# The subtractions that make the low parts of the HGRN weights, on VectorE in place of GpSimd

## The chip, the cores and the metric

One Trainium2 chip, of which the kernel uses one core. A core has five engines: TensorE (PE in the profile; PEld is its weight load), VectorE (DVE), ScalarE (ACT), GpSimd (POOL) and SyncE (SP), which issues most of the DMAs. Each takes its instructions in a fixed order. The metric is the device time of one execution in microseconds. Before the change it was 1303.19 us, the median of three runs.

## The reference

One layer of a hybrid decoder on 1024 tokens of width 1024. An RMS norm, one input projection, two groups of heads (8 HGRN heads of width 128, a gated linear recurrence; 16 FoX heads of width 64, softmax attention with a forget gate), a SiLU gate on each group, an output projection, a gated per-layer input, and a last norm.

```python
u = rmsnorm(h, norm_w[i])
proj = jnp.einsum('bsd,de->bse', u, w_in[i])
hq, hf, hi, hg, fq, fk, fv, fg, fz = jnp.split(proj, SPLIT_POINTS, axis=-1)
y_h = hgrn2_branch(hq, hf, hi, lb_all[i], hgrn_gn[i]) * jax.nn.silu(hg)
y_f = fox_branch(fq, fk, fv, fz, fox_fb[i]) * jax.nn.silu(fg)
h = h + jnp.einsum('bse,ed->bsd', jnp.concatenate([y_h, y_f], axis=-1), w_out[i])
ple = jnp.einsum('bsk,kd->bsd', p[i], w_ple[i])
h = h + jax.nn.sigmoid(jnp.einsum('bsd,de->bse', h, w_ple_gate[i])) * ple
```

`hgrn2_branch` keeps for each head a 128 x 128 state, S_t = diag(f_t) S_{t-1} + k_t i_t^T, with k = 1 - f, and reads it with q.

## The kernel before

**Products in split precision.** Each projection is a product of fp32 values in which both factors are split into a high part (rounded to the type fp32r) and a low part, and three of the four products of parts are summed: high x high, high x low, low x high. The helper `split` (L82, L83) makes the two parts of a tile: ScalarE casts the tile to its high part, then a second engine, given by the caller, subtracts that from the tile and so makes the low part. `load_w` (L88 the DMA) loads one tile of weights, 128 x 1024 fp32 (512 KB), into `wf` and splits it into `whi` and `wlo`; `load_pair` (L145) loads two such tiles for the values of a pair of heads into `wf` and splits them into the halves of `wthi` and `wtlo`. The tags `wf`, `whi` and `wlo` have two buffers each, `wthi` and `wtlo` one. So the cast of a tile waits until PE has done its last product with the tile two before, and the DMA of a tile waits until an earlier `wf` has been subtracted.

**The order of the loads** is written out in `w_in_loads`, a generator of closures: first the HGRN tiles (for each head f, q and g, with a pair of value tiles after every second head), then the FoX tiles, then the first tile of the output projection. `Ahead.weights()` hands out the tile that is loaded and starts the load of the next one, so each tile is loaded while the tile before it is multiplied. The numbers of the tiles are T_HQ 0 to 7, T_HF 8 to 15, T_HI 16 to 23, T_HG 24 to 31, and from T_FQ = 32 on the FoX tiles; a negative number stands for a pair. The first f tile and the first pair of value tiles are loaded elsewhere, in the start stage, by `load_w` and by `split_pair`, both with GpSimd.

**The HGRN stage** (about 55 to 520 us). For each of eight heads, `hgrn_mix` does the recurrence by blocks, and between its steps PE works ahead on the next head's projections: `ahead.fill(n)` runs so many columns of the jobs that are queued (`product_steps`, L371, the matmuls of 512 or 256 columns). PE's order is fixed as written (`pe` is `tc.keep_in_program_order`); the order on the other engines is made by the scheduler when the program is built, by what is ready and by the order of writing. The steps of a head that the prediction names:

- L579: PE's small matmuls for the scores of a group. L590, L591 and L621: VectorE copies them under a mask out of PSUM.
- L587, L596, L597, L614, L615, L635: VectorE scales the queries (`x`) for the next radix; L599, L645, L678, L681: it scales `k` and the queries. L599 and L645 stand ahead of the next scores (L579, then L661 and L673), L681 ahead of PE's transposes of `k` (L699). L633 is a copy on ScalarE.
- L699, L707, L726: PE transposes `k`, multiplies it with the values and makes the output; L711 and L713: VectorE's chain of states; L689: GpSimd copies the scores of the smallest blocks into `st`.
- L549, L552, L558 and L559: the projections for f, q and g leave PSUM; L559, on VectorE, multiplies the gate and frees the buffer. L562, L563: VectorE makes k and f from the sigmoid. L536: VectorE copies the values of one block out of PSUM. The projections have two PSUM buffers (the tag `proj`).
- L751 and L753: PE transposes a head's output and VectorE gates it.

Then comes the FoX stage (to about 1010 us), whose tiles are also loaded by `load_w` with GpSimd, and the output projection, whose tiles are split with VectorE.

Of the kernel before, what the change touches and what calls it, by code (L numbers as in the profile page):

```python
# [20 lines left out]
KT = D // P  # L21
CH = 512
NCH = S // CH
HEADS_H = 8
# [14 lines left out]
T_HQ, T_HF, T_HI, T_HG, T_FQ, T_FK, T_FV, T_FG = (8 * i for i in range(8))  # L39
# [25 lines left out]
def trunk(ctx: ExitStack, tc: tile.TileContext, a, out):  # L65
    nc = tc.nc
# [14 lines left out]
    def split(hi, lo, src, lo_engine, pin=lambda ins: ins):  # L81
        pin(nc.scalar.copy(hi, src))  # L82
        pin(lo_engine.tensor_tensor(out=lo, in0=src, in1=hi, op=ALU.subtract))  # L83

    def load_w(src, k, lo_engine=None, pin=lambda ins: ins):

        wf = wpool.tile([P, KT, P], F32, name="wf", tag="wf", bufs=2)
        nc.sync.dma_start(out=wf[:, :k], in_=src)  # L88
        hi = wpool.tile([P, KT, P], F32R, name="whi", tag="whi")
        lo = wpool.tile([P, KT, P], F32R, name="wlo", tag="wlo")  # L90
        split(hi[:, :k], lo[:, :k], wf[:, :k], lo_engine or nc.gpsimd, pin)
        return hi, lo
# [47 lines left out]
    def load_pair(tile0):  # L140

        whi, wlo = (wt.tile([P, KT, 2 * P], F32R, name=name) for name in ("wthi", "wtlo"))
        for i in range(2):
            wf = wpool.tile([P, KT, P], F32, name="wf", tag="wf", bufs=2)
            nc.sync.dma_start(out=wf, in_=a["w_in"][tile0 + i])  # L145
            sl = slice(i * P, (i + 1) * P)
            split(whi[:, :, sl], wlo[:, :, sl], wf, nc.gpsimd)
        return whi, wlo

    def token_major(w, v, blocks, evac_pin=lambda ins: ins):  # L150
# [232 lines left out]
    def w_in_loads():  # L383
        tiles = [T_HQ, T_HG]
        for h in range(HEADS_H - 1):
            tiles += [T_HF + h + 1, T_HQ + h + 1, T_HG + h + 1] + ([-(h + 2)] if h % 2 == 0 and h < HEADS_H - 2 else [])
        tiles += [T_FQ, T_FG, T_FK, T_FV]
        for p in range(PAIRS_F - 1):
            tiles += [T_FK + p + 1, T_FQ + p + 1] + ([T_FG + p] if 0 < p < FIRST_LATE else []) + [T_FV + p + 1]
        tiles += [T_FG + p for p in range(FIRST_LATE, PAIRS_F)]  # L390
        for t in tiles:
            yield (lambda t=t: load_w(a["w_in"][t], KT)) if t >= 0 else (lambda t=t: load_pair(T_HI - t))
        yield lambda: load_w(a["w_out"][0], KT, nc.vector)

    ahead = Ahead(w_in_loads(), first_f)


# [110 lines left out]
    with ExitStack() as st:  # L508
# [8 lines left out]
        for i in range(2):  # L517
            t = hs.tile([P, FB, P], F32, name=f"st{i}")
            nc.gpsimd.memset(t, 0.0)
            st_t.append(t)  # L520
            t = hs.tile([P, FB, 32], F32, name=f"r{i}")
# [261 lines left out]
    with fox as st:  # L783
# [219 lines left out]
        for c in range(NCH):  # L1003
            sl = slice(c * CH, (c + 1) * CH)
# [167 lines left out]
```

## Time and profile before

| what | us |
|---|---|
| time before, median of 3 runs (lowest, highest) | 1303.19 (1299.52, 1303.29) |
| the profiled execution's own time | 1302.99 |
| its span, from its first instruction to its last | 1301.2 |
| HGRN stage, 55 to 520 us: busy VectorE / ScalarE / GpSimd | 281.3 / 120.1 / 100.4 |
| FoX stage, 520 to 1010 us: busy PE / VectorE / GpSimd | 486.2 / 331.8 / 175.1 |

How to read the rows below. A row of the timeline gives the start in us, the duration in us, the engine, the line of the kernel, the operation, the tiles (out<-in), the shape, and how many instructions were merged (x2); in brackets the idle time of the engine just before and what ended it. A row of the waits gives who waited for whom: us in total, number of times, the longest in us. A row of a stretch gives from:to, its length and then the busy us of PE, PEld, DVE, ACT and POOL with the count of instructions, the granted share of PE's clock, the busy share of the DMA engines and GB/s. Durations in rows of a line (min/median/max) are in ns. A matmul's duration in the profile is longer than its step, since the next one starts before it ends; steps are read from start to start.

### The profile page before, as it was taken

The numbers are of one execution on the slowest core, as the hardware profiler recorded it, in microseconds if no ns is written. First come the engines' busy times: TensorE is split into PE (matmuls) and PEld (weight loads), VectorE is DVE, ScalarE is ACT, GpSimd is POOL, SyncE is SP. The second block draws the span as 40 slices with busy tenths as digits, with TensorE's granted clock in tenths as the row PEclk, the third lists the DMA queues.
The fourth block names the chain that finished last, engine by engine and source line by source line (L and its number), as shares of the span: only waits on it lengthen the run. The fifth ranks groups of instructions, "written<-read, shape, count | busy, mean of one in ns | idle before, by whom it ended". The sixth has DMA issues, their size and how long they took to land.

```text
span 1301.2 us, 26821 instructions
## 1 busy us (share of the span) xinstructions
PE 1263.7 (97%) x10996; PEld 1010.5 (78%) x10996; DVE 783.8 (60%) x1986; ACT 480.1 (37%) x1170; POOL 348.9 (27%) x288
## 2 busy tenths in 40 slices
PE   7998999999999999999999999999999999999996
PEld 5977888888788877777777777776766788888895
DVE  6555575755657486377666666667777633333465
ACT  6423132212313224255444444444545312222454
POOL 3522123212211112424343434242432100002232
PEclk9999999999999999999999999999999999999998
DMA  7411111101111020222122222211241652212321
GB/s 297 145 35 64 50 33 66 50 34 49 50 50 50 18 67 19 82 66 83 58 75 59 74 64 70 72 59 58 82 139 59 234 171 89 81 49 85 116 76 65
DMA packets 38971, 102.23 MB, mean 79 GB/s; under 512 B 6720, under 2 KB 8896, under 8 KB 38848
## 3 DMA queue, kind: packets, MB, share of 16 engines
q1 hardware_dynamic: 38704, 99.99, 23.2%
q8 instruction: 86, 1.41, 0.5%
q0 software_dynamic: 144, 0.52, 0.1%
q14 instruction: 37, 0.30, 0.1%
HBM read 83.07 MB, written 17.43 MB: 77 GB/s over the span
## 4 chain that ended last, share of the span: by engine, by line
PE 82%; DVE 7%; ACT 5%; DMA 2%; issue 2%; POOL 1%; SPq 0%; DVEq 0%; ACTq 0%; POOLq 0%
PE ps L371 47%; PE lg L828 5%; PE ps L100 5%; PE ps L98 5%; PE ps L99 5%; PE po L876 5%; ACT x L864 2%; PE ps L579 1%; PE gps L100 1%; PE gps L98 1%; PE gps L99 1%; DVE x L842 1%; PE po L724 1%; PE po L726 1%; PE pk L707 1%
## 5 line engine op out<-in xcount | busy, mean ns | idle before, releaser
L371 PE MATMUL ps<-uhi,whi 128*128 128x512 f32 x896 | 361.0, 403 | 0.0
L371 PE MATMUL ps<-ulo,whi 128*128 128x512 f32 x896 | 354.8, 396 | 0.0
L371 PE MATMUL ps<-uhi,wlo 128*128 128x512 f32 x896 | 353.1, 394 | 0.0
L83 POOL TENSOR_TENSOR wlo<-wf,whi 128x1024 fp32r<-128x1024 f32 x59 | 145.0, 2457 | 441.6 <-ACT whi L82 425.6
L371 PEld LDWEIGHTS ps<-uhi,whi 128*128 128x128 f32 x896 | 168.5, 188 | 58.4 <-issue 22.5
L371 PEld LDWEIGHTS ps<-uhi,wlo 128*128 128x128 f32 x896 | 168.9, 188 | 35.9 <-issue 1.1
L371 PEld LDWEIGHTS ps<-ulo,whi 128*128 128x128 f32 x896 | 168.8, 188 | 33.7 <-issue 0.7
L864 ACT ACTIVATE x<-x,mxo 128x512 f32<-128x512 f32 (+15 forms) x256 | 130.4, 512 | 66.0 <-DVE mxo L852 66.0
L82 ACT CAST whi<-wf 128x1024 fp32r<-128x1024 f32 (+1 forms) x77 | 79.7, 1036 | 202.2 <-PE ps L99 89.8
L842 DVE CUSTOM_DVE_ANT_0 x<-lg,fb 128x512 f32<-128x512 f32 (+15 forms) x256 | 101.8, 433 | 73.4 <-PE lg L828 66.6
L865 DVE STREAM_TRANSPOSE pt<-x 128x512 f32<-128x512 f32 (+15 forms) x256 | 115.1, 458 | 39.8 <-ACT x L864 35.9
L98 PE MATMUL ps<-yhi,whi 128*128 128x512 f32 x256 | 99.8, 390 | 1.7 <-DVE h L1024 1.7
L99 PE MATMUL ps<-ylo,whi 128*128 128x512 f32 x256 | 99.7, 389 | 0.3 <-DVE ylo L83 0.3
L100 PE MATMUL ps<-yhi,wlo 128*128 128x512 f32 x256 | 99.6, 389 | 0.0
L828 PE MATMUL lg<-k,q 64*32 64x480 f32 (+15 forms) x1024 | 74.9, 396 | 2.6 <-DVE mx L842 2.6
L828 PE MATMUL lg<-k,qx 64*32 64x512 f32 (+15 forms) x1024 | 74.9, 396 | 1.2 <-DVE mx L842 1.2
L876 PEld LDWEIGHTS po<-pt,v 64*64 64x64 f32 x1536 | 53.6, 133 | 22.7 <-issue 9.2
L876 PE MATMUL po<-pt,v 64*64 64x256 f32 (+7 forms) x1536 | 69.4, 320 | 0.0
L98 PEld LDWEIGHTS ps<-yhi,whi 128*128 128x128 f32 x256 | 48.0, 188 | 12.0 <-ACT whi L82 2.1
L99 PEld LDWEIGHTS ps<-ylo,whi 128*128 128x128 f32 x256 | 48.0, 188 | 10.7 <-DVE ylo L83 0.7
L100 PEld LDWEIGHTS ps<-yhi,wlo 128*128 128x128 f32 x256 | 48.1, 188 | 10.1
L371 PE MATMUL ps<-wthi,uhi 128*128 128x256 f32 x192 | 54.0, 281 | 0.0
(209 smaller groups left out, 2131.4 us busy)
## 6 DMA issues: line engine op xcount, KB each, us to landing
wf<-in_w_in_dram SPq DMA_DIRECT2D x64, 512.0 KB, 3.5
fb<-fd SPq DMA_DIRECT2D x64, 128.0 KB, 3.1
yf<-yd SPq DMA_DIRECT2D x16, 512.0 KB, 5.3
wf<-in_w_out_dram SPq DMA_DIRECT2D x16, 512.0 KB, 3.6
x<-in_xT_dram SPq DMA_DIRECT2D x8, 512.0 KB, 9.7
pled<-pleo SPq DMA_DIRECT2D x16, 256.0 KB, 3.0
yd<-sg SPq DMA_DIRECT2D x8, 512.0 KB, 2.6
rz<-zd SPq DMA_DIRECT2D x16, 256.0 KB, 3.4
```

The costliest lines, as they stand in the source:

```text
L82: pin(nc.scalar.copy(hi, src))
L83: pin(lo_engine.tensor_tensor(out=lo, in0=src, in1=hi, op=ALU.subtract))
L98: pin(mm(ps, whi, uhi, start=i == 0, stop=False))
L99: pin(mm(ps, whi, ulo, start=False, stop=False))
L100: pin(mm(ps, wlo, uhi, start=False, stop=i == n - 1))
L371: pe(mm(ps, x, y, start=i == j == 0, stop=i == n - 1 and j == 2))
L579: pe(mm(ps[32 * j : 32 * j + 32, c * 48 : c * 48 + 48], k[:, 32 * n : 32 * n + 32], mov(n), start=True, stop=True))
L828: mm(ps[32 * j : 32 * j + 32, m % 2, : 32 * n], q[:, 32 * (j // 2) :][:, :32], k[not own][rows].rearrange("p (t a k) -> p t a k", a=2, k=3 ...
L842: nc.vector.tensor_tensor_reduce(out=x, in0=ps[:, m % 2, : 32 * n], in1=copies[m % 2][:, : 32 * n], scale=1.0, scalar=BIG, op0=ALU.add, op ...
L864: nc.scalar.activation(x, x, AF.Exp, bias=self.other[:, g : g + 1], scale=-1.0, accum_out=zs[:, m : m + 1])
L865: nc.vector.transpose(self.probs[:, : m + 1, g], x.rearrange("p (t k) -> p t k", k=32))
L876: mm(po[half[t % 2], r, 32 * first : 256], v_t[self.p][half[r], t ^ r, half[self.i]], self.probs[half[r], t, first:].rearrange("p g q -> p ...
```

## The change

The engine that subtracts is VectorE in place of GpSimd for every weight tile of the HGRN stage that `w_in_loads` loads: the f, q and g tiles of the heads (all but the first f tile, 23 in number) and the three pairs of value tiles. The subtraction, its operands and its shape stay as they are, and so do the cast, the DMA and PE's order. The FoX tiles stay with GpSimd. The scheduler makes the order of VectorE's and GpSimd's instructions anew.

```diff
@@ -144,7 +144,7 @@ def load_pair(tile0):
             wf = wpool.tile([P, KT, P], F32, name="wf", tag="wf", bufs=2)
             nc.sync.dma_start(out=wf, in_=a["w_in"][tile0 + i])
             sl = slice(i * P, (i + 1) * P)
-            split(whi[:, :, sl], wlo[:, :, sl], wf, nc.gpsimd)
+            split(whi[:, :, sl], wlo[:, :, sl], wf, nc.vector)
         return whi, wlo
@@ -389,7 +389,9 @@ def w_in_loads():
         for t in tiles:
-            yield (lambda t=t: load_w(a["w_in"][t], KT)) if t >= 0 else (lambda t=t: load_pair(T_HI - t))
+            hgrn = t in (T_HQ, T_HG) or any(t - x in range(HEADS_H) for x in (T_HF, T_HQ, T_HG))
+            engine = nc.vector if hgrn else nc.gpsimd
+            yield (lambda t=t, engine=engine: load_w(a["w_in"][t], KT, engine)) if t >= 0 else (lambda t=t: load_pair(T_HI - t))
```

## The prediction

> **What bounds the kernel now.** I read the page first, for the shares of the engines.
>
> ```profile
> span 1301.2 us, 26821 instructions
> ## 1 busy us (share of the span) xinstructions
> PE 1263.7 (97%) x10996; PEld 1010.5 (78%) x10996; DVE 783.8 (60%) x1986; ACT 480.1 (37%) x1170; POOL 348.9 (27%) x288
> ```
>
> TensorE (PE) is busy 97% of the span, VectorE (DVE) 60%, GpSimd (POOL) 27%. So neither engine of the change is the bound, and the change can win only what PE loses by waiting for one of them in the HGRN stage. Next I asked for the busy times of that stretch, 55 to 520 us (the second number is PE's), and for whom PE waited in it, then for the one wait of several places in 200 to 340 us alone.
>
> ```profile
> 55.00:520.00 465.00, 455.00 (x4287) 385.78 (x4286) 281.32 (x615) 120.06 (x301) 100.36 (x70) 1.00 0.14 47
> ```
>
> ```profile
> PE ps L579 <- DVE k L599: 4.1, 4, 1.5
> PE pt L699 <- DVE k L681: 3.2, 1, 3.2
> PE pc L661 <- DVE k L645: 1.5, 2, 0.8
> ```
>
> ```profile
> PE ps L579 <- DVE k L599: 1.1, 2, 0.6
> ```
>
> PE is idle 465.0 - 455.0 = 10.0 us in the stage, and 8.8 of them are three kinds of wait for VectorE (total, times, longest). Waiting for VectorE would speak against giving it more work. So the third question was why VectorE is late at these seven places: the timeline of each engine around them. The subtractions themselves, on GpSimd from 60 to 460 us, and the same instruction where VectorE has it already:
>
> ```profile
> L83 POOL TENSOR_TENSOR wlo<-wf,whi x22: 2342/2403/2956, 72.1 to 451.4; 128x1024 fp32r<-128x1024 f32 x22
> L83 POOL TENSOR_TENSOR wtlo<-wf,wthi x6: 2411/2428/2554, 101.0 to 331.1; 128x1024 fp32r<-128x1024 f32 x6
> ```
>
> ```profile
> L83 DVE TENSOR_TENSOR wlo<-wf,whi x18: 691/1225/1226, 5.8 to 1174.1; 128x1024 fp32r<-128x1024 f32 x16, 128x512 fp32r<-128x512 f32 x2
> ```
>
> The durations are min/median/max in ns: 2.40 us on GpSimd, 1.225 us on VectorE. The 22 + 6 instructions, and the one for the tile T_HQ ahead of the window, are the 29 that move (23 single tiles, 3 pairs of 2). VectorE gets 29 x 1.225 = 35.5 us and GpSimd gives up some 29 x 2.40 = 70 us.
>
> **The worst place, head 0.** GpSimd, VectorE, ScalarE (ACT, which makes the high part ahead of each subtraction) and PE:
>
> ```profile
> 108.11 2.43 POOL L83 TENSOR_TENSOR wtlo<-wf,wthi 128x1024 fp32r<-128x1024 f32 x1 [1.25 <-ACT wthi L82]
> 110.96 2.34 POOL L83 TENSOR_TENSOR wlo<-wf,whi 128x1024 fp32r<-128x1024 f32 x1 [0.42 <-ACT whi L82]
> ```
>
> ```profile
> 108.91 2.18 DVE L678 TENSOR_TENSOR x<-x,t 128x512 f32<-128x512 f32 x1 [1.51 <-PE pd L673]
> 111.01 2.83 DVE L681 TENSOR_TENSOR k<-k,t 128x512 f32<-128x512 f32 x1
> ```
>
> ```profile
> 169.16 0.69 DVE L678 TENSOR_TENSOR x<-x,t 128x512 f32<-128x512 f32 x1 [1.71 <-PE pd L673]
> 169.77 0.68 DVE L681 TENSOR_TENSOR k<-k,t 128x512 f32<-128x512 f32 x1
> ```
>
> ```profile
> 113.90 1.06 PE L699 MATMUL pt<-cst,k 128*128 128x128 f32 x7 [3.23 <-DVE k L681]
> 114.64 0.76 PE L371 MATMUL ps<-uhi,whi 128*128 128x512 f32 x1
> ...
> 118.15 0.40 PE L371 MATMUL ps<-uhi,wlo 128*128 128x512 f32 x1
> ```
>
> L678 and L681 take 0.69 and 0.68 us in head 1, with no GpSimd subtraction beside them, and 2.18 and 2.83 us here. Each ends about one own duration (0.6) after GpSimd's instruction does: 108.91 + 2.18 = 111.09 against 108.11 + 2.43 = 110.54; 113.84 against 113.30. So an instruction of VectorE that reads two SBUF tiles stands still until a subtraction on GpSimd that began first is over. PE pays 3.23 us and then more: from 114.64 to 118.15 its eight steps of one 512-column matmul take 3.51 us, where an undisturbed stretch has 42 in 9.54 us (0.227 each, 1.82 for eight), and the granted clock of that stretch is 0.60:
>
> ```profile
> 113.90:118.20 4.30, 4.30 (x16) 3.57 (x17) 3.24 (x7) 0.97 (x2) 0.00 (x0) 0.60 0.40 122
> ```
>
> ```profile
> 126.70 9.54 PE ps L371 x42
> ```
>
> That is 1.7 us more. With the change the pair's subtraction starts on VectorE when its cast ends, and so does the tile's:
>
> ```profile
> 106.93 1.05 ACT L82 CAST wthi<-wf 128x1024 fp32r<-128x1024 f32 x1 [3.22 <-DMA wf<-in_w_in_dram]
> ...
> 109.83 1.05 ACT L82 CAST whi<-wf 128x1024 fp32r<-128x1024 f32 x1
> ```
>
> The first runs from 107.98 to 109.2, mostly in the 1.51 us in which VectorE was idle. L678 starts 0.3 late and L681 ends at about 110.5. The second is ready at 109.83 + 1.05 = 110.88, so it falls behind L681. PE came to L699 at 113.90 - 3.23 = 110.67. I count 3.1 of the 3.23 us as gone, and the 1.7 us of low clock with them: **4.8 us**. After the stall goes, PE's own order of matmuls is next.
>
> [...]
>
> **Before head 1's scores.** The rows of GpSimd, VectorE and PE at the end of the first three products:
>
> ```profile
> 93.90 2.39 POOL L83 TENSOR_TENSOR wlo<-wf,whi 128x1024 fp32r<-128x1024 f32 x1 [8.48 <-ACT whi L82]
> ```
>
> ```profile
> 93.59 3.00 DVE L635 TENSOR_TENSOR x<-x,t 128x256 f32<-128x256 f32 x2 [2.35 <-PE ps L579]
> ...
> 97.44 0.68 DVE L599 TENSOR_TENSOR k<-k,f 128x512 f32<-128x512 f32 x1
> ```
>
> ```profile
> 98.17 0.63 PE L579 MATMUL ps<-x,k 128*32 128x48 f32 x40 [1.49 <-DVE k L599]
> ```
>
> The two L635 take 3.00 us; 60 us later the same two take 0.76 (row at 155.45 below). 2.24 us are lost, and the subtraction in their place costs 1.23. So L599 comes 1.0 us sooner: **1.0 us** of the 1.49, or all of it if the subtraction is put behind L599.
>
> ```profile
> 155.45 0.76 DVE L635 TENSOR_TENSOR x<-x,t 128x256 f32<-128x256 f32 x2 [0.20 <-PE ps L579]
> ```
>
> **The two later pairs of value tiles** (200 to 340 us, two alike):
>
> ```profile
> 211.67 2.55 POOL L83 TENSOR_TENSOR wtlo<-wf,wthi 128x1024 fp32r<-128x1024 f32 x1 [9.09 <-ACT wthi L82]
> 218.83 2.41 POOL L83 TENSOR_TENSOR wtlo<-wf,wthi 128x1024 fp32r<-128x1024 f32 x1 [4.62 <-ACT wthi L82]
> ```
>
> ```profile
> 212.18 2.59 DVE L599 TENSOR_TENSOR k<-k,f 128x512 f32<-128x512 f32 x1
> ```
>
> L599 takes 2.59 in place of 0.68, 1.91 lost; even with 1.23 of subtraction ahead of it, it is done 0.7 sooner, and PE's wait there is 0.6 at most. At the second, L645 is held in the same way and PE waits 0.8 at most; the subtraction then begins at 218.8 on a VectorE that idles until PE's scores arrive, and is over by 220.0, where GpSimd held it to 221.2. I take both kinds whole: 1.1 + 1.5 = **2.6 us**. The fourth wait of L599 is not touched: by its time it follows the subtraction of a FoX tile, which stays on GpSimd.
>
> ```profile
> 484.17 0.54 PE L579 MATMUL ps<-x,k 128*32 128x48 f32 x30 [1.53 <-DVE k L599]
> ```
>
> **What the change adds.** In VectorE's queue, each subtraction waits for its cast, and that one for the end of PE's product of two tiles before, since the pool has two buffers. What queues behind it is VectorE's own mixing chain, for which PE waits. The place where it costs is the end of each gate tile:
>
> ```profile
> 143.33 1.05 ACT L82 CAST whi<-wf 128x1024 fp32r<-128x1024 f32 x1 [4.66 <-PE ps L371]
> ```
>
> ```profile
> 144.91 0.69 DVE L559 TENSOR_TENSOR sg<-ps,sg 128x512 f32<-128x512 f32 x1 [2.10 <-ACT sg L558]
> ```
>
> ```profile
> 146.14 0.28 PE L371 MATMUL ps<-wthi,uhi 128*128 128x256 f32 x1
> ```
>
> The cast ends at 144.38, the subtraction at 145.6, L559 then at 146.3 in place of 145.60. L559 frees one of the two PSUM buffers, and PE wants it for the second block of values at 146.14. So PE loses about 0.16 us, at the six heads whose gate tile is followed by values: **1.0 us**; nothing if the order puts L559 first. The other subtractions I cost at nothing. What hides them: those at the end of an f tile stand ahead of L562, which takes 2.77 us beside GpSimd in the row at 171.79 (in the last rival) where 1024 elements took 1.23 in a subtraction, and what follows L562 belongs to the next head, some 40 us ahead of PE's use of it. If that cover were gone the price would be up to 1.23 us at a place, and below nothing only by what VectorE gets back. No DMA changes its engine; SyncE's loads of the next tile may start 1.2 us sooner, since the buffer is free sooner.
>
> **The sum**, against the profiled execution (span 1301.2 us, its own time 1302.99, 0.2 under the median of 1303.19): 4.8 + 1.0 + 2.6 - 1.0 = 7.4 us. The median becomes 1303.2 - 7.4 = **1295.8 us**. Bounds of the terms: with the order best everywhere, 3.23 + 1.7 + 1.49 + 2.6 = 9.0; without the low clock, 7.4 - 1.7 = 5.7.
>
> **The rivals.**
>
> *The second subtraction of head 0 goes ahead of L681.* Then L681 ends at 110.88 + 1.23 + 0.68 = 112.8, PE waits 2.1 us in place of 3.23, and I let the low clock stay: the first term is 1.1 in place of 4.8, the sum 3.7, the time 1299.5. For it: the order is the scheduler's and not seen here. Against: L678 and L681 are ready first, and are written first.
>
> *No change.* VectorE is 60% busy and GpSimd 27%; if what VectorE gets back from the lock is only what it takes over, the waits stay as they are: 1303. For it: the sum of the work grows on the busier engine, by 35.5 us. Against: the four rows of 2.18 to 2.83 us, each 1.5 to 2.2 us too long, more than 1.23. [...]
>
> *Slower: head-of-line blocking in VectorE's queue.* In every other head the tile for the gate arrives just where L681 releases PE:
>
> ```profile
> 170.09 1.05 ACT L82 CAST whi<-wf 128x1024 fp32r<-128x1024 f32 x1 [0.18 <-issue]
> ```
>
> ```profile
> 171.79 2.77 DVE L562 TENSOR_SCALAR k<-k,oml 128x1024 f32<-128x1024 f32 x1 [1.33 <-ACT k L549]
> ```
>
> ```profile
> 170.77 0.93 PE L699 MATMUL pt<-cst,k 128*128 128x128 f32 x7
> ```
>
> The cast ends at 171.14. If the subtraction stands ahead of L678 and L681, PE's L699 waits until 171.14 + 1.23 + 0.69 + 0.68 = 173.74 in place of 170.77: 3.0 us at each of seven heads, 21 us, and the time is 1303.2 - 7.4 + 21 = 1316.8, without any low clock. It decides from three heads on (9.0 against the 7.4). Against it: L681 ends at 170.45, 0.7 us before the cast does, so an order by readiness has it first.
>
> **How the numbers follow.** About 0.3% (4 us, so below 1299.3) is what a measurement of this kernel can tell from no change. Forecast, with or without the low clock: 0.66. L681 second in head 0: 0.14, half of it faster and half the same. No change: 0.09. Slower: 0.11. So faster 0.73, same 0.16, slower 0.11. The range starts at 1292.5 (all of 9.0, and 1.7 for the spread of the runs before) and ends at 1301.0, past the first rival; it leaves out the last two.
>
> **What would show it.** On the changed profile: no L83 on GpSimd from 72 to 452 us; L562 well under 1.23 us; the wait for L681 gone, with the clock at 1.00 there; L599's waits down from 4.1 to about 2.0, of which 1.5 at 484 us; L645's gone; a few tenths of new wait at PE's value blocks behind L559. PE's idle time in the stage falls from 10.0 to about 4. If L699 waits in several heads for L681, the slower rival has it. If those waits vanish and the time stays, PE's waits were not what set the end.

## The result

The changed kernel takes 1294.59 us (median of 4 runs, 1294.21 to 1294.95), the kernel before 1303.21 in the same session; the ratio is 0.9938 (95% interval 0.9924 to 0.9953), 8.6 us or 0.66% less, where 7.4 was forecast. A second session gave 1294.24 and a ratio of 0.9931 (0.9919 to 0.9943). One thing is needed to read the numbers below: the times of the kernel before fall into two groups, near 1299.4 and near 1303.5 us (13 of 23 executions in the lower one in one session, where two more lie between, and 1 of 11 in another), and those of the changed kernel do not, so medians are compared with the changed kernel's 1294.4 and with the upper group unless an interval is given; against the lower group the gain is 5.0 us and not 8.6.

The page of the changed kernel, whose profiled execution took 1294.35 us:

```profile
span 1292.5 us, 26818 instructions
## 1 busy us (share of the span) xinstructions
PE 1259.8 (97%) x10996; PEld 1007.4 (78%) x10996; DVE 776.0 (60%) x2015; ACT 480.3 (37%) x1170; POOL 275.2 (21%) x259
```

VectorE took over 29 instructions of 1.225 us, 35.5 us, and is busy 776.0 in place of 783.8 us: it got back more than it took over. GpSimd gave up 73.7 us. The stretch of the stage (now 55 to 511 us, since the stage ends 9 us sooner), and whom PE waited for in it; the lines of the kernel have moved by two, so L599 is L601, L645 is L647, L681 is L683, L699 is L701:

```profile
55.00:511.00 456.00, 451.50 (x4285) 382.73 (x4283) 270.90 (x644) 120.07 (x301) 25.75 (x41) 1.00 0.15 48
```

```profile
PE pc L663 <- DVE k L647: 2.0, 2, 1.1
PE ps L581 <- DVE k L601: 1.5, 1, 1.5
PE pk L709 <- ACT kt L702: 0.5, 1, 0.5
PE pt L753 <- DVE o L746: 0.4, 1, 0.4
```

PE idles 4.5 us there in place of 10.0. The wait for L681 is gone, and of L599's four waits the one at 475 us is left, after a FoX tile. But L645's waits have grown from 1.5 to 2.0. The subtractions:

```profile
L83 DVE TENSOR_TENSOR wlo<-wf,whi x23: 1218/1226/2947, 52.3 to 442.5; 128x1024 fp32r<-128x1024 f32 x23
L83 DVE TENSOR_TENSOR wtlo<-wf,wthi x6: 1212/1225/1226, 99.5 to 323.3; 128x1024 fp32r<-128x1024 f32 x6
```

All but one take 1.21 to 1.23 us. The one of 2.947 us, at 52.3, runs while GpSimd still subtracts for the first f tile (51.74 to 54.14): the same hold, at a place where PE does not wait.

Head 0, VectorE and PE, and the clock of the stretch:

```profile
107.13 0.69 DVE L680 TENSOR_TENSOR x<-x,t 128x512 f32<-128x512 f32 x1 [0.37 <-PE pd L675]
107.74 0.69 DVE L683 TENSOR_TENSOR k<-k,t 128x512 f32<-128x512 f32 x1
109.10 1.23 DVE L83 TENSOR_TENSOR wlo<-wf,whi 128x1024 fp32r<-128x1024 f32 x1 [0.67 <-ACT whi L82]
```

```profile
108.74 0.49 PE L701 MATMUL pt<-cst,k 128*128 128x128 f32 x3
```

```profile
105.00:119.00 14.00, 14.00 (x98) 12.06 (x97) 10.23 (x24) 6.37 (x20) 0.00 (x0) 1.00 0.24 76
```

The two steps take 0.69 us each, the subtraction of the tile stands behind them as forecast, PE's row has no wait in brackets, and the clock is 1.00.

Ahead of the scores for which PE waited 1.49 us (the second of head 0's three groups, at 92.85, 98.17 and 101.75 in the trace of before; the prediction calls them head 1's):

```profile
93.64 1.23 DVE L83 TENSOR_TENSOR wlo<-wf,whi 128x1024 fp32r<-128x1024 f32 x1 [3.90 <-ACT whi L82]
94.79 0.68 DVE L561 TENSOR_TENSOR sg<-ps,sg 128x512 f32<-128x512 f32 x1
95.39 0.44 DVE L592 COPY_PREDICATED r<-masks,ps 128x256 f32<-128x256 int32 x1
95.72 0.68 DVE L601 TENSOR_TENSOR k<-k,f 128x512 f32<-128x512 f32 x1
```

```profile
96.45 0.25 PE L581 MATMUL ps<-x,k 128*32 128x48 f32 x4
```

L601 ends at 96.40, and PE comes to the scores at 96.45 and does not wait. The scheduler moved the two L635 from ahead of this chain to behind it.

Where the waits for L647 come from is read in four views, SyncE's loads of a pair, ScalarE's cast of its second tile, VectorE, PE:

```profile
193.97 13.53 SPq L145 DMA_DIRECT2D wf<-in_w_in_dram  x2
```

```profile
210.94 1.05 ACT L82 CAST wthi<-wf 128x1024 fp32r<-128x1024 f32 x1 [6.50 <-DMA wf<-in_w_in_dram]
```

```profile
205.92 1.22 DVE L83 TENSOR_TENSOR wtlo<-wf,wthi 128x1024 fp32r<-128x1024 f32 x1
...
212.02 1.23 DVE L83 TENSOR_TENSOR wtlo<-wf,wthi 128x1024 fp32r<-128x1024 f32 x1 [2.61 <-ACT wthi L82]
213.16 0.37 DVE L623 COPY_PREDICATED r<-masks,ps 128x192 f32<-128x192 int32 x1
```

```profile
214.99 0.22 PE L663 MATMUL pc<-x,k 128*32 128x32 f32 x2 [1.12 <-DVE k L647]
```

The second load of the merged row is issued at about 207.2 (193.97 + 13.53 = 207.50 is its end), when the first tile's subtraction has freed the buffer; the cast waits for it; VectorE stands still for 2.61 us ahead of the subtraction, and L623 and L647, whose scores PE has finished at about 211.2, stand behind.

### The profile page after: what moved, and what is told of

Its sections match the earlier page's. It is cut to its first block, busy times and chain, and to the rows that moved or that the text cites. A ratio compares the mean times of both kernels' runs of the same rounds, so it can differ in the third digit from the quotient of the medians.

```text
span 1292.5 us, 26818 instructions
## 1 busy us (share of the span) xinstructions
PE 1259.8 (97%) x10996; PEld 1007.4 (78%) x10996; DVE 776.0 (60%) x2015; ACT 480.3 (37%) x1170; POOL 275.2 (21%) x259
## 4 chain that ended last, share of the span: by engine, by line
PE 83%; DVE 6%; ACT 5%; DMA 3%; issue 2%; POOL 1%; SPq 0%; DVEq 0%; ACTq 0%; POOLq 0%
PE ps L371 47%; PE lg L830 5%; PE ps L100 5%; PE ps L98 5%; PE ps L99 5%; PE po L878 5%; ACT x L866 2%; PE gps L100 1%; PE gps L99 1%; PE gps L98 1%; DMA wf<-in_w_in_dram 1%; PE ps L581 1%; DVE x L844 1%; PE po L726 1%; PE pk L709 1%
## 5 line engine op out<-in xcount | busy, mean ns | idle before, releaser
L844 DVE CUSTOM_DVE_ANT_0 x<-lg,fb 128x512 f32<-128x512 f32 (+15 forms) x256 | 101.8, 433 | 73.7 <-PE lg L830 66.9
L83 POOL TENSOR_TENSOR wlo<-wf,whi 128x1024 fp32r<-128x1024 f32 x36 | 86.7, 2408 | 246.4 <-ACT whi L82 218.0
L691 POOL TENSOR_SCALAR st<-r 32x256 f32<-32x256 f32 x32 | 14.6, 455 | 377.2 <-DVE r L623 375.4
L83 DVE TENSOR_TENSOR wlo<-wf,whi 128x1024 fp32r<-128x1024 f32 (+1 forms) x41 | 50.8, 1240 | 42.8 <-ACT whi L82 42.8
```

Of the source, the lines that this page charges most:

```text
L691: nc.gpsimd.tensor_scalar(out=stt[sl, :, sl], in0=r[sl], scalar1=1.0, scalar2=1.0, op0=ALU.mult, op1=ALU.mult)
L844: nc.vector.tensor_tensor_reduce(out=x, in0=ps[:, m % 2, : 32 * n], in1=copies[m % 2][:, : 32 * n], scale=1.0, scalar=BIG, op0=ALU.add, op ...
```

## The experiments

| run | what | us, median (lowest, highest) | ratio to before, 95% interval |
|---|---|---|---|
| e1_head0 | 4 subtractions of head 0's product moved | 1296.55 (1296.00, 1296.83) | 0.9959 (0.9945, 0.9973) |
| e2_rest | the other 25 moved | 1300.73 (1296.43, 1301.22) | 0.9992 (0.9978, 1.0006) |
| e3_read | all moved, GpSimd reads beside them | 1309.08 (1307.53, 1310.91) | 1.0055 (1.0033, 1.0077) |
| e4_write | all moved, GpSimd fills beside them | 1294.87 (1294.65, 1295.54) | 0.9946 (0.9925, 0.9967) |
| after_again | the changed kernel | 1294.24 (1293.84, 1294.74) | 0.9931 (0.9919, 0.9943) |
| e5_fox3 | and three FoX tiles | 1292.58 (1291.98, 1292.99) | 0.9918 (0.9904, 0.9931) |
| e6_stage | and a staging buffer for pairs | 1292.35 (1291.92, 1292.62) | 0.9916 (0.9903, 0.9929) |
| e7_both | both of these | 1290.12 (1289.71, 1290.39) | 0.9899 (0.9886, 0.9912) |
| e9_hg1 | before, one subtraction moved | 1300.10 (1299.04, 1301.28) | 0.9981 (0.9972, 0.9990) |
| e10_fill | before, and one fill more on GpSimd | 1299.50 (1299.27, 1300.03) | 0.9973 (0.9964, 0.9982) |

The first four share a session in which the kernel before had a median of 1299.78 us, the lower group; in the others it was 1303.3 to 1303.6. The changed kernel itself was not run in that session, which was on another chip, so its 1294.4 is carried over from the other sessions.

**Which subtractions make the gain.** First only those that arrive around head 0's steps:

```diff
-            split(whi[:, :, sl], wlo[:, :, sl], wf, nc.vector)
+            split(whi[:, :, sl], wlo[:, :, sl], wf, nc.vector if tile0 == T_HI + 2 else nc.gpsimd)
-            hgrn = t in (T_HQ, T_HG) or any(t - x in range(HEADS_H) for x in (T_HF, T_HQ, T_HG))
+            hgrn = t in (T_HQ + 1, T_HG + 1)
```

> Only the tiles that arrive between head 0's gate product and head 1's value blocks are moved to VectorE: the query and gate tiles of head 1 and the first pair of value tiles (4 subtractions of the 29; the first query and gate tile of the stage move too early to matter and stay on GpSimd). Theory A, that the gain is the end of the lock by which GpSimd holds VectorE's chain just where PE waits for that chain: the wait of 1.5 us before the first scores, the wait of 3.2 us before the transposes of head 0 and the 1.7 us of low clock go, some 6.5 us of the 8.6, so about 1296.8. Rival B, that each low part is ready 1.2 us sooner and the load of the next tile starts sooner, so that all 29 count about alike: 4/29 of 8.6 = 1.2 us, about 1302. Rival C, that GpSimd's queue is relieved: also in proportion, about 1302.

1296.55 us: with 4 of 29 moved, the time is 2.1 us above the changed kernel's. The complement, with the two conditions turned round:

```diff
+            split(whi[:, :, sl], wlo[:, :, sl], wf, nc.gpsimd if tile0 == T_HI + 2 else nc.vector)
+            hgrn = t in (T_HQ, T_HG) or t not in (T_HQ + 1, T_HG + 1) and any(t - x in range(HEADS_H) for x in (T_HF, T_HQ, T_HG))
```

> The complement: the 25 other subtractions on VectorE, those 4 on GpSimd. Theory A: the 3.2 us wait at head 0 and its low clock are back, and so are most of the 1.5 us before it; about 2 us gained, about 1301. Rivals B and C: 25/29 of the gain, about 1295.8. The profile tells also whether a stall of some 3 us is followed by a low clock a second time (1.7 us) or not.

1300.73 us, 6.3 above the changed kernel. Its profile has head 0's stall again, and the low clock for a second time; the 1.5 us ahead of the scores are back too. Whom PE waited for, VectorE's instruction, and the clock behind it:

```profile
PE pt L701 <- DVE k L683: 3.3, 1, 3.3
```

```profile
110.62 2.83 DVE L683 TENSOR_TENSOR k<-k,t 128x512 f32<-128x512 f32 x1
```

```profile
113.80:117.20 3.40, 3.40 (x13) 2.91 (x12) 2.94 (x7) 1.07 (x2) 0.00 (x0) 0.50 0.47 154
```

So, counted from the upper group, 4 subtractions bring about three quarters of the gain and 25 the rest. That rules out B and C as they were stated.

**Is it the lock, and what takes it?** The changed kernel with work on GpSimd beside each moved subtraction. It leaves out nothing of the computation; the extra result goes into a tile of its own.

```diff
+    def beside(hi):
...
+        nc.gpsimd.tensor_tensor(out=spare, in0=hi, in1=hi, op=ALU.subtract)
```

> The changed kernel, and beside each moved subtraction GpSimd also runs one of the same shape on the high part alone, into a spare tile that nobody reads. The low part is ready as soon as in the changed kernel, and the weight buffer is free as soon. Theory A: GpSimd holds VectorE again, now after the subtraction's own 1.23 us, so the waits of PE for L601, L647 and L683 come back and are longer than before: 1300 to 1312. Rival B: nothing changes, about 1294.6. Rival C: GpSimd's queue is as full as before, about 1303.

1309.08 us, 14.7 above the changed kernel, though VectorE's subtractions still take 1.21 to 1.23 us each in the stage (all but the one at 52.3). PE's longest waits, GpSimd and VectorE behind head 0's gate tile:

```profile
PE po L738 <- DVE state L723: 7.8, 3, 2.6
```

```profile
113.05 4.52 POOL L89 TENSOR_TENSOR spare<-wthi 128x1024 f32<-128x1024 f32 x2
```

```profile
111.14 2.38 DVE L574 TENSOR_SCALAR k<-k,oml 128x1024 f32<-128x1024 f32 x1
113.56 2.27 DVE L575 TENSOR_SCALAR f<-k 128x1024 f32<-128x1024 f32 x1
115.86 2.27 DVE L613 TENSOR_TENSOR t<-f 128x512 f32<-128x512 f32 x1
```

Three instructions that take 0.75, 0.69 and 0.69 us otherwise take 2.3 us each, one behind each instruction of GpSimd, and the chain of states behind them is 2.6 us late for PE. The size and the sign are as theory A had it; the place is another: three waits for the states, none for L683, while those for L601 and L647 grow by 0.8 and 0.4 us only. Then the same with fills, which read nothing:

```diff
+    def beside(hi):
...
+        nc.gpsimd.tensor_tensor(out=spare[:, 0], in0=hi[:, 0], in1=hi[:, 0], op=ALU.subtract)
+        for _ in range(2):
+            nc.gpsimd.memset(spare, 0.0)
```

> As the last, but GpSimd's extra work is a small subtraction of 128 x 128 from the high part and then two fills of the spare tile, 0.95 us each in the profile before, so about as long and hardly reading. [...] If GpSimd holds VectorE whatever it does: 1300 or more. Rival C: about 1303.

1294.87 us, the changed kernel's time within 0.6. GpSimd, then VectorE, at two places:

```profile
93.73 1.37 POOL L89 TENSOR_TENSOR spare<-whi 128x128 f32<-128x128 f32 x1 [7.47 <-ACT whi L83]
95.16 1.97 POOL L91 MEMSET spare<- 128x1024 f32 x2
...
110.72 2.82 POOL L91 MEMSET spare<- 128x1024 f32 x2
```

```profile
95.69 0.68 DVE L613 TENSOR_TENSOR k<-k,f 128x512 f32<-128x512 f32 x1
...
111.24 1.40 DVE L577 TENSOR_SCALAR f<-k 128x1024 f32<-128x1024 f32 x1
112.68 0.69 DVE L615 TENSOR_TENSOR t<-f 128x512 f32<-128x512 f32 x1
```

L613 and L615 read two SBUF inputs each and run their 0.68 and 0.69 us beside the fills (L615 at seven heads). L577, with one input, takes 1.40 in place of 0.69 at all eight heads, and in the rows shown the two fills take 2.82 in place of 1.97. So what held these instructions with two inputs is GpSimd's reading: L613 of e3_read, the line that is L615 here, took 2.27 us beside a reading instruction.

**One subtraction alone, from the side of the kernel before.**

```diff
-            yield (lambda t=t: load_w(a["w_in"][t], KT)) if t >= 0 else ...
+            yield (lambda t=t: load_w(a["w_in"][t], KT, nc.vector if t == T_HG + 1 else None)) if t >= 0 else ...
```

> The kernel before with one subtraction of the 29 moved: the gate tile of head 1, the one beside which L681 takes 2.83 us in head 0. L678 is still held by the pair's subtraction, until 111.1; then L681 takes 0.68 and PE's wait for it falls from 3.2 to about 1.1 us, too short for a low clock. Theory A: 2.1 + 1.7 = 3.8 us, about 1299.3 where the kernel before has 1303, and no spread of 4 us between executions. Rivals B and C: 1/29 of 8.6, 0.3 us.

1300.10 us against 1303.32, all eleven executions within 2.3 us of one another; PE's wait for L681 is 1.1 us in its profile, and the clock stays at 1.00, as it does in the kernel before at the 1.49 us wait for L599 (98 to 102 us). One subtraction of 29 brings 3.2 us of the 8.6 that the upper group is above the changed kernel. Two more profiles of the kernel before were to tell what its lower group is:

> The kernel before as it is. Its times fell into two groups, near 1299.3 and near 1303 to 1304. One look with a profile: if the time is near 1299.3, either the low clock after head 0's stall is missing (then the wait for L681 is 3.2 us still and the time 1.7 us lower), or L681 has begun ahead of GpSimd's subtraction, which it misses by 0.05 us in the first profile (then the wait is about 1.1 us, and there is no low clock: 3.8 us lower).

> The same once more, for another execution of the two groups.

Both came out in the upper group (1303.19 and 1303.09), with the wait of 3.2 and 3.4 us and the low clock. The lower group was not profiled. So I asked the question from the other side: GpSimd is given a fill ahead of this one subtraction (`fill` is set for head 1's gate tile alone), so that it begins to subtract after L681 has begun.

```diff
+        if fill:
+            nc.gpsimd.memset(lo.bitcast(F32), 0.0)
         split(hi[:, :k], lo[:, :k], wf[:, :k], lo_engine or nc.gpsimd, pin)
```

> The kernel before, all subtractions on GpSimd, and ahead of the one for head 1's gate tile GpSimd also fills that low part with zeros (0.95 us by the profile, reading nothing). So GpSimd does more work and this low part is ready about 0.5 us later, but the subtraction now begins after L681 has begun. Theory A, the lock goes to who begins first: L681 takes about 0.7 us, PE waits about 1.1 in place of 3.2 us, no low clock, and the time is that of the run with this one subtraction moved, about 1300, in one group. Rivals B and C (the low part's delay, GpSimd's load): no faster than the kernel before, or a little slower, 1303 in two groups.

1299.50 us, 3.9 below the kernel before, with all subtractions on GpSimd and a fill more. GpSimd and VectorE:

```profile
111.13 0.95 POOL L92 MEMSET wlo<- 128x1024 f32 x1
112.16 2.43 POOL L83 TENSOR_TENSOR wlo<-wf,whi 128x1024 fp32r<-128x1024 f32 x1
```

```profile
111.67 0.68 DVE L683 TENSOR_TENSOR k<-k,t 128x512 f32<-128x512 f32 x1
112.27 2.88 DVE L564 TENSOR_SCALAR k<-k,oml 128x1024 f32<-128x1024 f32 x1
```

L683 (L681 before) began 0.49 us ahead of the subtraction and ran its 0.68; the next instruction, L564, was held instead, at 2.88 us in place of 0.74, and PE does not wait for it. PE's wait for L683 is 1.3 us and the clock stays at 1.00. A later low part and a busier GpSimd made the kernel faster, so neither the low part's date nor GpSimd's load was the price here; who begins first was. In the three profiles of the kernel before, GpSimd wins that race by 0.05 us (110.96 against 111.01), 0.07 and 0.23, and in e2_rest by 0.13. That executions in which it loses make up the lower group fits its level, 1299.4, and its absence in the kernels that take this subtraction out of the race; e2_rest, which leaves it there, has one execution of twelve at 1296.43, 4.3 below its median. No execution of a lower group was profiled, so this is argued and not shown.

**What is left in the stage.** The three FoX tiles that are subtracted inside it, on VectorE too:

```diff
+            hgrn = t in (T_HQ, T_HG, T_FQ, T_FG, T_FK) or any(t - x in range(HEADS_H) for x in (T_HF, T_HQ, T_HG))
```

> The changed kernel once more, to stand beside the next three on the same chip: 8.6 us below the kernel before.

> The changed kernel, and the first three FoX tiles (query, gate, and the second key tile), whose subtractions fall into the HGRN stage, on VectorE too. Theory A: the wait of 1.5 us for L601 at 475 us goes, as the same wait in head 0 did, and the 0.4 us for L746 at 509 us: 1.5 to 1.9 us below the changed kernel. Rivals B and C: 3/29 of 8.6, below 0.9 us.

1292.58 us, 1.7 below the changed kernel beside it: the wait of 1.5 us and that of 0.4 are gone from its list. Then the head-of-line blocking at the pairs:

```diff
-            wf = wpool.tile([P, KT, P], F32, name="wf", tag="wf", bufs=2)
+            wf = (stage[0] if i else wpool).tile([P, KT, P], F32, name="wf", tag="wf", bufs=1 if i else 2)
```

> The changed kernel, with a staging buffer of its own for the second tile of each pair of value tiles, so that its load need not wait for the first tile's subtraction. In the changed kernel PE waits 1.1 and 0.9 us for L647 where VectorE stands behind the second subtraction, that behind its cast, and that behind the load. Theory D, head-of-line blocking by the late load: both waits go, up to 2.0 us below the changed kernel. Rival, that VectorE just has 1.23 us too much to do there: two subtractions stand together and the waits stay, 0 us.

1292.35 us, 1.9 below. VectorE, with both subtractions of the pair merged in one row (lines moved by three):

```profile
205.98 2.35 DVE L83 TENSOR_TENSOR wtlo<-wf,wthi 128x1024 fp32r<-128x1024 f32 x2
208.25 0.44 DVE L626 COPY_PREDICATED r<-masks,ps 128x192 f32<-128x192 int32 x1
```

They stand one behind the other without a pause, and PE's waits for L647 are gone. VectorE does the same work there; only the late load was the price.

> Both of the last two. If the two are independent their gains add: 3.5 to 3.9 us below the changed kernel, about 1291.

1290.12 us, 4.1 below the changed kernel and 13.4 below the kernel before in the same session (ratio 0.9899); the two gains alone are 1.7 and 1.9, so they add up, with 0.5 to spare. Its stage, 55 to 507 us:

```profile
55.00:507.00 452.00, 451.46 (x4290) 383.13 (x4290) 267.98 (x647) 121.35 (x302) 17.00 (x38) 1.00 0.14 47
```

PE is idle 0.5 us there, all of it one wait for ScalarE (L705), and nothing is left in this stage for this mechanism.

## Why the prediction was right

*Head 0, 4.8 us forecast.* Right. From its second scores to the products with the values (L707, now L709) the distance between the two traces grows from 1.7 us (98.17 against 96.45) to 6.8 (118.38 against 111.59), 5.1 us: 3.4 of wait and 1.6 of clock. Before, then after:

```profile
118.38 1.72 PE L707 MATMUL pk<-v,kt 128*128 128x128 f32 x14
```

```profile
111.59 1.72 PE L709 MATMUL pk<-v,kt 128*128 128x128 f32 x14
```

VectorE's order was the one counted on. Run e9 and run e10 show the larger half alone: L681 unheld, 3.2 and 3.9 us.

*The wait before the scores, 1.0 forecast.* All of the 1.49 came. The step that gave 0.5 too little took the two L635 to stay ahead of the chain; the new order has them behind it.

*The pairs, 2.6 forecast.* Half right. L599's 1.1 us went; at L645 the 1.5 us did not go but became 2.0. The step that failed is "the subtraction then begins at 218.8 on a VectorE that idles until PE's scores arrive, and is over by 220.0": it took the date of the cast from the trace of before, and that cast waits for a load that waits for the first tile's subtraction. I had named what queues behind a waiting subtraction, and not followed its own wait back to SyncE's queue. In the trace of before the second load was issued when GpSimd was done with the first tile, and the mixing chain did not stand behind it, since it was another engine that waited. The first tile's subtraction now also has the mixing chain ahead of it in VectorE's queue: its cast ends at 204.13 and it begins at 205.92. Counted from PE's first scores of the head, the second cast now begins at 7.97 us (7.27 before), and the third scores, which L623 copies, at 7.30 (7.97 before), since L599's wait is gone. That the late load is the price e6_stage shows: with the load free of that wait both waits are gone. So the term was about 0.6 by the waits, in place of 2.6.

*The price at the gate tiles, 1.0 forecast.* It came, and something that the prediction did not have paid it back. VectorE copies the values of one block at L536 (now L538) as soon as PE has made it, so the distance from copy to copy is PE's time for a block. Before, then after:

```profile
146.34 0.42 DVE L536 COPY v<-ps 128x256 f32<-128x256 f32 x1 [0.74 <-PE ps L371]
149.17 0.42 DVE L536 COPY v<-ps 128x256 f32<-128x256 f32 x1 [2.40 <-PE ps L371]
152.00 0.42 DVE L536 COPY v<-ps 128x256 f32<-128x256 f32 x1 [2.40 <-PE ps L371]
```

```profile
139.54 0.42 DVE L538 COPY v<-ps 128x256 f32<-128x256 f32 x1
142.51 0.43 DVE L538 COPY v<-ps 128x256 f32<-128x256 f32 x1 [2.54 <-PE ps L371]
145.23 0.43 DVE L538 COPY v<-ps 128x256 f32<-128x256 f32 x1 [2.29 <-PE ps L371]
```

Each block took 2.83 us. Now the second takes 2.97, since its first step comes late, behind L561 (it starts at 139.46, 0.24 us after the step before it), and those after it 2.72: PE's steps of 256 columns go down from 0.118 us to 0.113. Over the six heads the second blocks lose 0.85 us (five times 0.12 to 0.14, and 0.22 at the sixth); at five heads the faster steps win back a little more, and at the sixth they stay at 0.118. The net is 0.2 us gained. In after_again and e6_stage the second block takes 2.95 us and the next two 2.72 at all six heads; in e1_head0, where these subtractions stay on GpSimd, every block takes 2.82 or 2.83. So the late start and the faster steps come together; why a late start makes the steps shorter, no run here shows.

*The sum*, by the distance between the two traces at PE's instructions: 5.1 at head 0, 1.5 at the scores, 0.8 at the two later pairs and 0.2 at the value blocks. The forecast had no term for the rest: 0.2 is there at 48 us, from the start stage; 0.5 comes at the output of head 1 (L724, L726), where PE no longer waits 0.2 us for VectorE's chain of states; 0.5 in all comes at the outputs of heads 2 to 5, 0.1 to 0.2 each, without a wait in the list. That makes 8.8; the spans differ by 8.7. So the largest term and its mechanism were right, and that the sum came out near is in part luck: the pairs gave 1.8 less than forecast, and the gate tiles and the outputs together about 2 more. The choice of the group helped too: against the lower one the gain is 5.0 us, and if e10_fill shows what the lower group is, most of head 0's term is missing from it.

*The rivals.* "L681 second" did not come, by VectorE's rows. "No change" fell with VectorE's busy time, which went down by 7.8 us while it took on 35.5; L562 (now L564), 2.77 us in the prediction's row, takes 0.75 in the mean of the eight heads. The slower one, head-of-line blocking in VectorE's queue, is real: it came at another place, at two of the three pairs and not at the seven gate tiles, and cost 2.0 us and not 21.

*The low clock.* It followed head 0's stall in all four profiles that have a stall of 3.2 us or more there (the three of the kernel before, and e2_rest; 0.60 or 0.61 from 113.9 to 118.2 us). The prediction's bound without it, 5.7 us, takes a stall of 3.23 us with no low clock behind it, and no profile shows one.

## What to carry to other kernels

An engine that is neither the bound nor late by its own work can still be the one that holds the bound: ask of each late step of VectorE whether a GpSimd instruction that reads SBUF runs beside it, and compare its duration with the same step elsewhere (L681: 2.83 us beside one, 0.68 without). Moving such work to VectorE pays where the hold costs more than the work itself (here 1.5 to 2.2 us against 1.23), and at the few places where the critical engine waits: 4 of 29 made three quarters of the gain. Where it is one place, delaying the other engine can do as well: one fill of 0.95 us ahead of one subtraction brought 3.9 us. A moved instruction takes its waits along, so follow them back to the load, since everything behind it in the new queue will stand there too.

## What the runs showed of the hardware that was not expected

The one that began first held the other, in both directions: VectorE's L681 began 0.05 us behind GpSimd's subtraction in the kernel before and took 2.83 us in place of 0.68, and a 128 x 128 subtraction on GpSimd that begins 0.11 us behind VectorE's 1.22 us one takes 1.37 us in e4_write and ends 0.26 us behind it (95.10 against 94.84), where the same takes 0.47 us alone (at 113.61). In the kernel before, GpSimd is first by 0.05 to 0.23 us at L681, and turning that order round is worth 3.9 us (e10_fill).

The low clock needs no stall of 3.2 us. In e3_read PE waits 2.60 us at three places; behind the first, at 118.8 us, the clock stays at 1.00, behind the others, at 234.4 and 350.0, it falls:

```profile
117.00:121.00 4.00, 2.16 (x14) 2.02 (x15) 3.97 (x15) 0.00 (x0) 0.57 (x1) 1.00 0.00 0
233.00:238.00 5.00, 3.58 (x15) 3.36 (x16) 4.62 (x17) 0.32 (x2) 0.15 (x1) 0.66 0.01 3
349.00:354.00 5.00, 4.01 (x16) 3.70 (x17) 4.18 (x17) 0.72 (x4) 0.00 (x0) 0.66 0.00 0
```

So 2.60 us of wait were followed by a low clock at two places of three. The waits are of equal length and the outcome differs; what decides it, no run here shows.
